# Score operands of a hybrid decoder step: which head's tiles the engines write and which the DMA moves fill, and when the cache copies are issued

## The chip, the cores and the metric

The kernel runs on one core of one Trainium2 chip. The metric is the device time of one execution in microseconds (us). The profile shows one further execution, engine by engine. The engines are TensorE (PE), VectorE (DVE), ScalarE (ACT), GpSimd (POOL) and SyncE (SP); here SP's queue issues all DMA transfers, in program order, and a transfer that has to wait holds up all that are behind it.

## The reference

One step of a one-layer decoder: 1024 prompt positions and 8 decode sequences, width 1024. One projection gives q, k and v of three dilated attention groups (8 heads of 64 each, dilations 1, 4 and 16), of one sliding-window group with a sink, and four gate paths. The caches, one position moved on, are outputs too.

```python
def layer_prompt(x, norm_gain, w_in, ...):
    a_qkv, (bq, bk, bv), gates = project_inputs(x, norm_gain, w_in, qk_norm_a, qk_norm_b)
    for g in range(A_GROUPS):                       # windows 128, 512, 2048; dilations 1, 4, 16
        q, k, v = a_qkv[g]
        o, lse = dilated_prompt(q, k, v, A_WINDOWS[g], A_DILATIONS[g])
        ...
    o_b, _ = banded_attention(bq, bk, bv, alibi_slopes(B_HEADS, 1), b_sinks, B_WINDOW, 1)
    y = merge_branches(x, jnp.stack(o_list), jnp.stack(lse_list), o_b, gates, w_branch_a, w_branch_b, w_out)

def decode_attention(q, cache_kv, k_new, v_new, n_keys, dil, slopes, sinks, window):
    kk = jnp.concatenate([cache_kv[:, :, 0], k_new], axis=1)
    ...
    new_kv = jnp.stack([kk[:, -keep:], vv[:, -keep:]], axis=2)      # the cache, moved on by one row

def merge_branches(x, o_a_groups, lse_a, o_b, gates, ...):
    wts = jax.nn.softmax(lse_a, axis=0)             # the three groups, by their softmax denominators
    o_a = jnp.einsum("gnth,gnthd->nthd", wts, o_a_groups)
    a = o_a.reshape(n, t, A_WIDTH) * jax.nn.silu(z_a)
    b = o_b.reshape(n, t, B_WIDTH) * jax.nn.silu(z_b)
    mixed = sigmoid(g_a) * (a @ w_branch_a) + sigmoid(g_b) * (b @ w_branch_b)
    return x + mixed @ w_out
```

## The kernel before

The work is a list of 82 weight tiles of 128 output columns (ORDER): gate tiles, then q, k and v tiles of the groups with gates between them, then the z tiles (58 to 65), the branch tiles (66 to 73) and the output tiles (74 to 81). Each tile is computed for 1032 columns (1024 prompt positions and 8 decode sequences) in three column blocks of 344. A column block is a slot of 24 matmuls, issued in three parts of 8 (line 248). Every operand is split into a high and a low part, and a product is high by high, high by low and low by high. The weights of tile n+2 are loaded by SP (line 118) while ACT and POOL split those of n+1 (lines 126 and 127).

Between the parts the program puts attention work: part_end runs what was put off by `after(parts, f)`, which means f runs that many parts later. A part is 8 projection matmuls plus the attention pieces put beside it, some 1.3 to 2 us. So the order of all queues is written out by these numbers, and nothing reorders it.

A q or k tile holds two heads, one in partitions 0 to 63 (lo_rows), the other in 64 to 127 (hi_rows). The score matmul of a head contracts over 128 partitions: a head's q tile holds its high part in one half and its low part in the other, and the k tiles are laid against it. So each part must be had by both heads' tiles, one in the place where it is written, the other by a DMA `move` of 64 partitions (256 KB, line 311; 128 KB in the dilation-16 group, line 348). prep_q fills q0 and q1 (both named q_st) for the two heads. prep_k fills, for head 0, a0 and b0, and for head 1, a1 and b1 (a named k_a and b k_b). It is used by the sliding-window group, once for all heads, and by the groups of dilation 1 and 4, once for each of their four tiles, nine times in all; prep_k2 does the same for dilation 16 with tiles k_st.

The score matmuls of a head against a and b are lines 448 and 449 (line 434 for dilation 16). One unit of score work is issued in every third part, all units of head 0 ahead of those of head 1: four units a head, two in the dilation-16 group. In stage_s line 457 (DVE) and line 467 (ACT) make the softmax numerators of a unit.

merge weighs the three groups of a head pair in four column quarters: DVE multiplies one group (line 726), POOL the other two and adds them (line 729), DVE adds the sum (line 731), and SP stores it (line 735). The z tiles read it back, and DVE multiplies it in (lines 1122, 1123). `yield n` lets n parts pass.

cache_copies moves the caches on by one row, from DRAM to DRAM, in 89 pieces: 64 of 1020 KB or a little more for the largest cache, 16 of that size for the next, 8 of 508 KB, and one of 1016 KB (line 145). slot issues one at the end of every second slot until they are used up, and a loop behind the last slot issues what is left. In the output tiles, ev_out loads the residual (xres, line 1172), DVE adds it (line 1174), and SP stores (line 1175).

Of the kernel before, what the change touches and what calls it, by code (L numbers as in the profile page):

```python
# [10 lines left out]
F32 = mybir.dt.float32  # L11
# [3 lines left out]
ALU = mybir.AluOpType  # L15
# [52 lines left out]
def hybrid_step(ctx: ExitStack, tc: tile.TileContext, a):  # L68
# [244 lines left out]
    def prep_q(j):  # L313

        j.sq = [rt("q_st") for _ in range(2)]
        t = rt("q_lo")
        q0, q1 = j.sq

        def piece(half):
            c = part_of(j, half)  # L320
            v = j.view(j.q[:, :T])[:, c]
            h = j.view_o(q0[:, :T])[:, c]
            nc.scalar.activation(h, v, AF.Copy)
            nc.gpsimd.tensor_tensor(j.view_o(t[:, :T])[:, c], v, h.bitcast(F32), op=ALU.subtract)  # L324
            if half:
                after(1, lambda: move(q1, lo_rows, q0, hi_rows))
                after(3, lambda: move(q1, hi_rows, t, hi_rows))
                after(3, lambda: move(q0, hi_rows, t, lo_rows))

        return [lambda: piece(0), lambda: piece(1)]  # L330

# [4 lines left out]
    def prep_k2(j):  # L336

        j.sk = [[rt("k_st") for _ in range(2)] for _ in range(2)]

        def piece(y):  # L340
            v = j.k[:, :T].rearrange("p (s r) -> p r s", r=16)[:, 8 * y:8 * y + 8].rearrange("p (b w) s -> p b w s", w=2)
            t0, t1 = [side(j.sk[h][y]) for h in range(2)]
            t4 = t0.rearrange("p b l (w s) -> p b l w s", s=64)
            nc.scalar.activation(t4[:, :, 0], v, AF.Copy)
            nc.vector.tensor_tensor(t4[:, :, 1], v, t4[:, :, 0].bitcast(F32), op=ALU.subtract)

            def mv(dst, d, l, src, s, m):
                nc.sync.dma_start(dst[d, :, l].bitcast(F32), src[s, :, m].bitcast(F32))

            after(1, lambda: mv(t1, lo_rows, 0, t0, hi_rows, 0))  # L350
            after(1, lambda: mv(t1, hi_rows, 1, t0, hi_rows, 0))
            after(2, lambda: mv(t1, lo_rows, 1, t0, hi_rows, 1))
            after(2, lambda: mv(t1, hi_rows, 0, t0, hi_rows, 1))
            after(5, lambda: mv(t0, hi_rows, 1, t0, lo_rows, 0))
            after(5, lambda: mv(t0, hi_rows, 0, t0, lo_rows, 1))

        return [lambda: piece(0), lambda: None, lambda: piece(1)]

    def prep_k(j):

        j.ka = [rt("k_a0"), rt("k_a1")]
        j.sk = [rt("k_b0"), rt("k_b1")]
        (a0, a1), (b0, b1) = j.ka, j.sk

        def piece(half):
            c = part_of(j, half)
            v = j.view(j.k[:, :T])[:, c]
            h = j.view_o(a0[:, :T])[:, c]
            nc.scalar.activation(h, v, AF.Copy)
            nc.vector.tensor_tensor(j.view_o(b0[:, :T])[:, c], v, h.bitcast(F32), op=ALU.subtract)  # L370
            if half:
                after(1, lambda: move(a1, lo_rows, a0, hi_rows))
                after(1, lambda: move(b1, hi_rows, a0, hi_rows))
                after(2, lambda: move(a1, hi_rows, b0, hi_rows))
                after(2, lambda: move(b1, lo_rows, b0, hi_rows))
                after(5, lambda: move(b0, hi_rows, a0, lo_rows))
                after(5, lambda: move(a0, hi_rows, b0, lo_rows))

        return [lambda: piece(0), lambda: None, lambda: piece(1)]

# [272 lines left out]
    def merge(c, js):  # L653
# [58 lines left out]
        for quarter in range(4):  # L712
            sc = scs[quarter]
            c0 = 256 * quarter
            for x, j in enumerate(js):
                if j.g == 1:
                    nv = j.n[:, :T].rearrange("p (r i) -> p i r", r=4)[:, 64 * quarter:64 * quarter + 64]
                    sv = sc[:, x].rearrange("p (i r) -> p i r", r=4)
                elif j.g == 2:
                    nv = j.n[:, :T].rearrange("p (r s) -> p s r", r=16)[:, 16 * quarter:16 * quarter + 16]  # L720
                    sv = sc[:, x].rearrange("p (s r) -> p s r", r=16)
                else:
                    nv = j.n[:, c0:c0 + 256]
                    sv = sc[:, x]
                eng = nc.vector if x == 0 else nc.gpsimd
                eng.tensor_tensor(nv if x == 0 else sv, nv, sv, op=ALU.mult)  # L726
            nv = js[0].n[:, c0:c0 + 256]
            if G == 3:
                nc.gpsimd.tensor_tensor(sc[:, 1], sc[:, 1], sc[:, 2], op=ALU.add)
                yield 2  # L730
                nc.vector.tensor_tensor(nv, nv, sc[:, 1], op=ALU.add)
            yield
            if quarter < 2:
                load(quarter + 2)
            nc.sync.dma_start(o_dr[oc, :, c0:c0 + 256], nv)
            yield 1
# [458 lines left out]
    def slot(n, ch):  # L1195
# [21 lines left out]
        else:  # L1217
            evac(n, ch, pt)
        part_end(in_att)
        if now[0] % 6 == 0 and now[0] > 18:  # L1220
            next(copies, None)

    n_tail = ORDER.index(("br", 0, 0))
# [254 lines left out]
```

## Time and profile before

| | |
|---|---|
| median of 3 runs | 1248.19 us (1246.03 to 1253.07) |
| profiled execution | 1248.59 us, its span 1246.0 us |
| busy: PE, ACT, DVE, POOL | 1181.5, 730.4, 707.0, 606.3 us |
| mean granted clock of PE | 0.977 of full speed |
| moved by DMA | 238.83 MB, 192 GB/s over the span |

Busy times are of the span of 1246.0 us. The span goes from the first to the last instruction; the profiled execution's own time has 2.6 us more around it. The granted clock is the share of full speed (2.4 GHz) that PE was given; its other level is half of it. The engine named behind an arrow in the profile is what ended a wait; "issue" stands where the profile shows nothing that did.

### The profile page before, as it was taken

Reading aid. Unit: us, or ns where it says so; the run is one execution under the profiler, and the core shown is the slowest. Engines: PE = TensorE matmul, PEld = TensorE weight load, DVE = VectorE, ACT = ScalarE, POOL = GpSimd, SP = SyncE. Lnnn points to the kernel's source line nnn. Section 1 sums busy time; section 2 is a strip of 40 time slices with the busy share of each in tenths; the row PEclk is TensorE's granted clock in tenths of the full one; section 3 lists DMA queues with packets and bytes.
Section 4 is the critical chain, followed back from the end, with each engine's and each line's share of the span. In section 5 each row is a group of like instructions: output and inputs, shape, how many; then the busy total and the mean of one; then the engine's idle time right before and its main releaser. Section 6 shows DMA issues by size and latency. Waiting matters only on the chain.

```text
span 1246.0 us, 21929 instructions
## 1 busy us (share of the span) xinstructions
PE 1181.5 (95%) x7625; PEld 1154.4 (93%) x7625; DVE 707.0 (57%) x1714; ACT 730.4 (59%) x1830; POOL 606.3 (49%) x681
## 2 busy tenths in 40 slices
PE   7899999999999998989998989989899999999998
PEld 6799999999899988979987989989899989999998
DVE  5852454676667475766755865757855564333111
ACT  5644675776758584758755677847686522443110
POOL 3554243443535455746363853638554685444220
PEclk9999999999999998989998989989999998999999
DMA  7047557675684849667775859486688754543343
GB/s 224 35 145 224 175 195 223 195 228 149 221 266 166 254 145 279 194 168 220 213 227 177 241 191 264 143 262 195 182 258 228 238 178 161 187 145 110 111 147 100
DMA packets 127278, 238.83 MB, mean 192 GB/s; under 512 B 28648, under 2 KB 102208, under 8 KB 125760
## 3 DMA queue, kind: packets, MB, share of 16 engines
q1 hardware_dynamic: 127168, 237.43, 62.3%
q8 instruction: 60, 0.98, 0.3%
q14 instruction: 50, 0.41, 0.1%
HBM read 180.14 MB, written 113.25 MB: 235 GB/s over the span
## 4 chain that ended last, share of the span: by engine, by line
PE 73%; DMA 7%; DVE 6%; POOL 5%; ACT 4%; issue 4%; SPq 1%; POOLq 0%; DVEq 0%; ACTq 0%
PE ps_d L248 55%; PE ps_w L248 4%; DMA k_a<-k_b 3%; PE ps_w L501 3%; PE ps_o L574 2%; PE ps_w L448 2%; PE ps_w L449 2%; DMA k_b<-k_b 2%; DMA w_st<-in_w 1%; ACT P L467 1%; PE ps_o L248 1%; DVE n_t L726 1%; POOL q_lo L324 1%; POOL n_t L591 1%; PE ps_w L950 1%
## 5 line engine op out<-in xcount | busy, mean ns | idle before, releaser
L248 PE MATMUL ps_d<-h_hi,w 128*128 128x344 f32 x3456 | 867.7, 327 | 12.2 <-DVE sq L1122 5.7
L248 PEld LDWEIGHTS ps_d<-h_hi,w 128*128 128x128 f32 x3456 | 611.7, 193 | 17.1 <-ACT h_hi L191 6.7
L248 PE MATMUL ps_d<-h_lo,w 128*128 128x344 f32 x1728 | 573.2, 332 | 5.9 <-POOL h_lo L221 3.3
L248 PEld LDWEIGHTS ps_d<-h_lo,w 128*128 128x128 f32 x1728 | 332.2, 192 | 10.6 <-POOL h_lo L221 5.8
L127 POOL TENSOR_TENSOR w<-w_st,w 128x512 fp32r<-128x512 f32 (+1 forms) x159 | 211.1, 1330 | 208.3 <-ACT w L126 193.4
L126 ACT ACTIVATE w<-w_st 128x512 fp32r<-128x512 f32 (+1 forms) x160 | 100.3, 631 | 113.3 <-DMA w_st<-in_w 112.5
L467 ACT ACTIVATE P<-P,st 128x256 f32<-128x256 f32 (+1 forms) x256 | 115.6, 453 | 65.6 <-DVE st L457 59.4
L956 POOL TENSOR_TENSOR qn<-qn,rn 128x344 f32<-128x344 f32 x48 | 45.6, 949 | 151.6 <-ACT rn L226 139.7
L528 DVE TENSOR_TENSOR pt<-ps_w,pt 128x384 fp32r<-128x384 f32 (+1 forms) x112 | 49.4, 441 | 57.7 <-ACT pt L527 57.3
L448 PE MATMUL ps_w<-k_a,q_st 128*128 128x128 f32 (+1 forms) x192 | 51.8, 293 | 29.0 <-DMA k_a<-k_b 14.6
L527 ACT ACTIVATE pt<-ps_w 128x384 fp32r<-128x384 f32 (+1 forms) x112 | 44.1, 394 | 42.8 <-DVE pt L528 36.0
L448 PEld LDWEIGHTS ps_w<-k_a,q_st 128*128 128x128 f32 x192 | 37.6, 196 | 31.0 <-issue 31.0
L501 PE MATMUL ps_w<-ident,P 128*128 128x128 f32 x400 | 62.3, 273 | 3.9 <-DVE pt L528 2.1
L956 POOL TENSOR_TENSOR kn<-kn,rn 128x344 f32<-128x344 f32 x39 | 37.0, 949 | 57.0 <-ACT rn L226 51.8
L941 ACT ACTIVATE sq<-ps_d 128x344 f32<-128x344 f32 x87 | 39.3, 452 | 39.8 <-PE ps_d L248 36.2
L946 DVE TENSOR_TENSOR sql<-sq,sqh 128x344 fp32r<-128x344 f32 x87 | 59.5, 684 | 0.8
L457 DVE CUSTOM_DVE_ANT_0 P<-ps_w,tab 128x256 f32<-128x256 f32 (+1 forms) x128 | 43.4, 375 | 27.4 <-PE ps_w L449 27.2
L501 PEld LDWEIGHTS ps_w<-ident,P 128*128 128x128 f32 x400 | 50.2, 140 | 7.1 <-issue 2.3
L792 POOL TENSOR_TENSOR dkv<-dkv,qb 128x512 f32<-128x512 f32 x32 | 42.4, 1331 | 28.0 <-DMA dkv<-in_ca 9.5
L1174 DVE TENSOR_TENSOR xres<-ps_d,xres 128x344 f32<-128x344 f32 x24 | 12.4, 517 | 76.1 <-PE ps_d L248 44.9
L230 DVE SCALAR_TENSOR_TENSOR ps_w<-ps_w,rt 128x344 f32<-128x344 f32 x87 | 45.2, 520 | 18.0 <-ACT rt L227 17.7
L449 PE MATMUL ps_w<-k_b,q_st 128*128 128x128 f32 (+1 forms) x192 | 53.1, 287 | 0.0
(226 smaller groups left out, 2064.7 us busy)
## 6 DMA issues: line engine op xcount, KB each, us to landing
w_st<-in_w SPq DMA_DIRECT2D x81, 512.0 KB
out_sa<-in_ca SPq DMA_DIRECT2D x16, 1020.0 KB
dkv<-in_ca SPq DMA_DIRECT2D x24, 512.0 KB
q_st<-q_lo SPq DMA_DIRECT2D x32, 256.0 KB
k_st<-k_st SPq DMA_DIRECT2D x48, 128.0 KB
sc<-sc_dr SPq DMA_DIRECT2D x32, 192.0 KB
k_b<-k_a SPq DMA_DIRECT2D x18, 256.0 KB
k_a<-k_b SPq DMA_DIRECT2D x18, 256.0 KB
```

The lines of the kernel that those rows point to most:

```text
L126: nc.scalar.activation(wh, s, AF.Copy)
L127: eng.tensor_tensor(wl, s, wh.bitcast(F32), op=ALU.subtract)
L230: nc.vector.scalar_tensor_tensor(ssq, ssq, n * EPS, t, op0=ALU.add, op1=ALU.mult)
L248: nc.tensor.matmul(pt[:, :CH], ops[i][0], ops[i][1], start=(i == 0), stop=(i == N - 1))
L448: nc.tensor.matmul(pt[:, o:o + 128 * nk], j.sq[h][:, q], j.ka[h][:, k], start=True, stop=False)
L449: nc.tensor.matmul(pt[:, o:o + 128 * nk], j.sq[h][:, q], j.sk[h][:, k], start=False, stop=True)
L467: nc.scalar.activation(u.p[:, c], u.p[:, c], AF.Exp, scale=-1.0, bias=st[:, qb, h:h + 1], accum_out=st[:, qb, 2 + h:3 + h])
L501: nc.tensor.transpose(pt[:, o:o + 128], u.p[:, o:o + 128], ident)
L527: nc.scalar.activation(t[:, p0:p0 + m], pt[:, o:o + m], AF.Copy)
L528: nc.vector.tensor_tensor(t[:, 512 + p0:512 + p0 + m], pt[:, o:o + m], t[:, p0:p0 + m].bitcast(F32), op=ALU.subtract)
L946: after(0, lambda: nc.vector.tensor_tensor(sl, s, sh.bitcast(F32), op=ALU.subtract))
L956: nc.gpsimd.tensor_tensor(dst[:, col], dst[:, col], r, op=ALU.mult)
```

## The change

In prep_q, prep_k and prep_k2 the tiles change roles: ACT's high part and the subtraction's low part are written to tiles of the second head (in prep_q the high part to a tile of its own, now q_hi), and the moves are turned about, so that the first four (in prep_q the first two) fill the first head's tiles and the last two (the last one) complete the second's. These last moves are issued 7 parts on instead of 5 (3 in prep_q). In merge the last add comes 3 parts behind POOL's instead of 2. The cache copies are issued every 9 parts up to tile 58 and every 6 parts from there on.

```diff
@@ def prep_q(j):
-        t = rt("q_lo")
+        t = rt("q_hi")
         q0, q1 = j.sq
...
-            h = j.view_o(q0[:, :T])[:, c]
+            h = j.view_o(t[:, :T])[:, c]
             nc.scalar.activation(h, v, AF.Copy)
-            nc.gpsimd.tensor_tensor(j.view_o(t[:, :T])[:, c], v, h.bitcast(F32), op=ALU.subtract)
+            nc.gpsimd.tensor_tensor(j.view_o(q1[:, :T])[:, c], v, h.bitcast(F32), op=ALU.subtract)
             if half:
-                after(1, lambda: move(q1, lo_rows, q0, hi_rows))
-                after(3, lambda: move(q1, hi_rows, t, hi_rows))
-                after(3, lambda: move(q0, hi_rows, t, lo_rows))
+                after(1, lambda: move(q0, lo_rows, t, lo_rows))
+                after(3, lambda: move(q0, hi_rows, q1, lo_rows))
+                after(7, lambda: move(q1, lo_rows, t, hi_rows))
@@ def prep_k(j):   (prep_k2 in the same way, with 7 for 5)
-            h = j.view_o(a0[:, :T])[:, c]
+            h = j.view_o(b1[:, :T])[:, c]
             nc.scalar.activation(h, v, AF.Copy)
-            nc.vector.tensor_tensor(j.view_o(b0[:, :T])[:, c], v, h.bitcast(F32), op=ALU.subtract)
+            nc.vector.tensor_tensor(j.view_o(a1[:, :T])[:, c], v, h.bitcast(F32), op=ALU.subtract)
             if half:
-                after(1, lambda: move(a1, lo_rows, a0, hi_rows))
-                after(1, lambda: move(b1, hi_rows, a0, hi_rows))
-                after(2, lambda: move(a1, hi_rows, b0, hi_rows))
-                after(2, lambda: move(b1, lo_rows, b0, hi_rows))
-                after(5, lambda: move(b0, hi_rows, a0, lo_rows))
-                after(5, lambda: move(a0, hi_rows, b0, lo_rows))
+                after(1, lambda: move(a0, lo_rows, b1, lo_rows))
+                after(1, lambda: move(b0, hi_rows, b1, lo_rows))
+                after(2, lambda: move(a0, hi_rows, a1, lo_rows))
+                after(2, lambda: move(b0, lo_rows, a1, lo_rows))
+                after(7, lambda: move(a1, lo_rows, b1, hi_rows))
+                after(7, lambda: move(b1, lo_rows, a1, hi_rows))
@@ merge, the last add of a quarter
-                yield 2
+                yield 3
                 nc.vector.tensor_tensor(nv, nv, sc[:, 1], op=ALU.add)
@@ def slot(n, ch):
-        if now[0] % 6 == 0 and now[0] > 18:
+        if now[0] % (9 if n < n_tail - 8 else 6) == 0 and now[0] > 18:
             next(copies, None)
```

SP's queue before, at the second k tile of the dilation-4 group (the numbers at k_a and k_b tell the tiles apart: 6313 and 6314 are a0 and a1, 6315 and 6316 are b0 and b1):

```order
L311 DMA k_a_6314<-k_a_6313 64x1024
L311 DMA k_b_6316<-k_a_6313 64x1024
L311 DMA k_a_6314<-k_b_6315 64x1024
L311 DMA k_b_6316<-k_b_6315 64x1024
L970 DMA out_pa<-v_t 128x512
L735 DMA o_dr<-n_t 128x256
L141 DMA out_sa<-in_ca 16x16384
L311 DMA k_b_6315<-k_a_6313 64x1024
L311 DMA k_a_6313<-k_b_6315 64x1024
L118 DMA w_st<-in_w 128x1024
```

The same place in the changed kernel (6296 and 6297 are a0 and a1, 6298 and 6299 are b0 and b1):

```order
L311 DMA k_a_6296<-k_b_6299 64x1024
L311 DMA k_b_6298<-k_b_6299 64x1024
L141 DMA out_sa<-in_ca 16x16384
L311 DMA k_a_6296<-k_a_6297 64x1024
L311 DMA k_b_6298<-k_a_6297 64x1024
L970 DMA out_pa<-v_t 128x512
L706 DMA sc<-sc_dr 64x3x256 x2
L735 DMA o_dr<-n_t 128x256
L311 DMA k_a_6297<-k_b_6299 64x1024
L311 DMA k_b_6299<-k_a_6297 64x1024
L118 DMA w_st<-in_w 128x1024
```

The first head's tiles are now filled by the first four moves instead of by the last two, a cache copy stands ahead of the third, and the one that stood ahead of the last two is gone.

The end of SP's queue before, the last two output tiles:

```order
L1172 DMA xres<-in_xT 128x1032
L1175 DMA out_yT<-xres 128x344 x3
L1172 DMA xres<-in_xT 128x1032
L1175 DMA out_yT<-xres 128x344 x3
L1474 UNCONDITIONAL_BRANCH
```

And in the changed kernel:

```order
L141 DMA out_sa<-in_ca 16x8128
L1172 DMA xres<-in_xT 128x1032
L1175 DMA out_yT<-xres 128x344 x2
L141 DMA out_sa<-in_ca 16x8128
L1175 DMA out_yT<-xres 128x344
L1172 DMA xres<-in_xT 128x1032
L1175 DMA out_yT<-xres 128x344
L141 DMA out_sa<-in_ca 16x8128
L1175 DMA out_yT<-xres 128x344 x2
L141 DMA out_sa<-in_ca 16x8128
L145 DMA out_sb<-in_cb 16x8x2032
L1474 UNCONDITIONAL_BRANCH
```

Copies of 508 KB now stand among the residual loads and stores, and the last two copies behind the last store.

## Rows read from the trace of the kernel before

**Rows 1.** The page: busy us and share by engine; DMA's busy tenths in 40 slices.
```profile
PE 1181.5 (95%) x7625; PEld 1154.4 (93%) x7625; DVE 707.0 (57%) x1714; ACT 730.4 (59%) x1830; POOL 606.3 (49%) x681
...
DMA  7047557675684849667775859486688754543343
```

**Rows 2.** PE's waits: line, releaser, us in total, times, longest.
```profile
PE ps_w L448 <- DMA k_a<-k_b: 14.6, 4, 6.0
PE ps_w L448 <- issue: 14.3, 4, 5.3
PE ps_d L248 <- DVE sq L1122: 5.7, 2, 3.0
```

**Rows 3.** PE's timeline at three of these waits: start, us, instruction, [idle before].
```profile
316.16 0.44 PE L448 MATMUL ps_w<-k_a,q_st 128*128 128x128 f32 x1 [2.99 <-DMA k_a<-k_b]
...
549.42 0.44 PE L448 MATMUL ps_w<-k_a,q_st 128*128 128x128 f32 x1 [6.00 <-DMA k_a<-k_b]
...
664.99 0.45 PE L448 MATMUL ps_w<-k_a,q_st 128*128 128x128 f32 x1 [5.31 <-issue]
```

**Rows 4.** SP's queue, timeline of 523 to 552 us.
```profile
533.72 0.60 SPq L311 DMA_DIRECT2D k_b<-k_b  x1
...
538.80 0.47 SPq L311 DMA_DIRECT2D k_b<-k_a  x1
539.36 1.53 SPq L311 DMA_DIRECT2D k_a<-k_b  x1
```

**Rows 5.** SP's queue, timelines of 300 to 312 and 648 to 668 us.
```profile
309.81 0.46 SPq L311 DMA_DIRECT2D k_b<-k_a  x1
...
652.86 0.60 SPq L311 DMA_DIRECT2D k_b<-k_b  x1
...
660.66 0.46 SPq L311 DMA_DIRECT2D k_b<-k_a  x1
```

**Rows 6.** SP's own waits, whole span: us in total, times, longest.
```profile
SPq L311 <- DMA k_b<-k_b: 24.2, 9, 6.3
```

**Rows 7.** Windows behind two waits; columns: us, PE, PEld, DVE, ACT, POOL, PEclk, DMA, GB/s.
```profile
491.75:498.75 7.00, 7.00 (x30) 6.61 (x31) 2.28 (x8) 2.65 (x8) 1.28 (x1) 0.63 0.87 329
834.73:839.73 5.00, 5.00 (x23) 5.00 (x24) 1.71 (x7) 1.69 (x6) 1.29 (x1) 0.66 1.10 447
```

**Rows 8.** The window of the wait that ends at 664.99.
```profile
660.00:665.00 5.00, 0.01 (x1) 0.04 (x1) 0.00 (x0) 0.49 (x1) 0.91 (x1) 0.92 0.64 154
```

**Rows 9.** SP's queue, timeline of 1040 to 1060 us: the last two copies.
```profile
1046.79 0.52 SPq L141 DMA_DIRECT2D out_sa<-in_ca  x1
1047.36 0.61 SPq L145 DMA_DIRECT2D out_sb<-in_cb  x1
```

**Rows 10.** Windows behind these copies.
```profile
1048.00:1050.00 2.00, 2.00 (x15) 2.00 (x14) 0.00 (x0) 0.39 (x1) 0.95 (x1) 1.00 1.16 451
1054.00:1056.00 2.00, 2.00 (x14) 2.00 (x14) 1.03 (x2) 0.82 (x3) 0.45 (x1) 1.00 0.00 0
```

**Rows 11.** SP's queue, timeline of 1243 to 1246 us.
```profile
1243.07 0.33 SPq L1175 DMA_DIRECT2D out_yT<-xres  x1
```

**Rows 12.** DVE's timeline of 1230 to 1246 us, the last output tile.
```profile
1236.18 0.52 DVE L1174 TENSOR_TENSOR xres<-ps_d,xres 128x344 f32<-128x344 f32 x1 [4.47 <-DMA xres<-in_xT]
1238.74 0.52 DVE L1174 TENSOR_TENSOR xres<-ps_d,xres 128x344 f32<-128x344 f32 x1 [2.04 <-PE ps_d L248]
```

**Rows 13.** SP's and ACT's timelines, 1090 to 1110 us: a gate's load and use.
```profile
1094.71 0.32 SPq L1149 DMA_DIRECT2D sg<-ga_dr  x1
...
1104.91 2.01 ACT L1155 ACTIVATE sg<-sg 128x1032 f32<-128x1032 f32 x2
```

**Rows 14.** DVE's timeline of 1005 to 1042 us, a multiply of the last merge.
```profile
1011.64 6.40 DVE L726 TENSOR_TENSOR n_t<-n_t,sc 128x256 f32<-128x256 f32 x1
```

**Rows 15.** PE's timeline of 1013 to 1020 us.
```profile
1018.51 0.43 PE L248 MATMUL ps_d<-h_hi,w 128*128 128x344 f32 x1 [2.97 <-DVE sq L1122]
```

**Rows 16.** The merge's last add, line 731: ns min/median/max; what its engine waited for.
```profile
L731 DVE TENSOR_TENSOR n_t<-n_t,sc x16: 404/792/3405, 514.8 to 1035.2; 128x256 f32<-128x256 f32 x16
...
  POOL sc L729: 2.9, 2
```

More of the change, by code (lines that the diff above doesn't have):

```diff
@@ L342, in piece @@
             t0, t1 = [side(j.sk[h][y]) for h in range(2)]
-            t4 = t0.rearrange("p b l (w s) -> p b l w s", s=64)
-            nc.scalar.activation(t4[:, :, 0], v, AF.Copy)
-            nc.vector.tensor_tensor(t4[:, :, 1], v, t4[:, :, 0].bitcast(F32), op=ALU.subtract)
+            t4 = t1.rearrange("p b l (w s) -> p b l w s", s=64)
+            nc.scalar.activation(t4[:, :, 1], v, AF.Copy)
+            nc.vector.tensor_tensor(t4[:, :, 0], v, t4[:, :, 1].bitcast(F32), op=ALU.subtract)
             def mv(dst, d, l, src, s, m):
                 nc.sync.dma_start(dst[d, :, l].bitcast(F32), src[s, :, m].bitcast(F32))
[L350 to L355, printed above, removed]
+            after(1, lambda: mv(t0, lo_rows, 0, t1, lo_rows, 1))
+            after(1, lambda: mv(t0, hi_rows, 1, t1, lo_rows, 1))
+            after(2, lambda: mv(t0, hi_rows, 0, t1, lo_rows, 0))
+            after(2, lambda: mv(t0, lo_rows, 1, t1, lo_rows, 0))
+            after(7, lambda: mv(t1, lo_rows, 0, t1, hi_rows, 1))
+            after(7, lambda: mv(t1, lo_rows, 1, t1, hi_rows, 0))
         return [lambda: piece(0), lambda: None, lambda: piece(1)]
```

## The prediction, made before the changed kernel was run

> **What bounds the kernel now.** I read the page first. TensorE (PE) is busy in 1181.5 of 1246.0 us and no other engine in more than 59% [rows 1], so the time falls only if PE's idle time falls or its clock rises. The profiled execution took 1248.59 us for its span of 1246.0 us, so 2.6 us lie around the span; the median of the runs is 1248.19 us, the same within 0.4 us, and the sum below is made from 1248.6.
>
> Next the waits of PE, longest first. The largest are two rows of one line, L448, the first score matmul of a head: 14.6 us in four waits put down to the move k_a<-k_b, and 14.3 us in four for which the view names no releaser [rows 2]. Together 28.9 us in eight waits, nearly half of PE's 64.5 us of idle time. To see what a wait "issue" is, I set PE's timeline against SP's queue, which issues the transfers. At 543.4 PE stops and goes on at 549.42, after 6.00 us [rows 3]. SP issued k_b<-k_b at 533.72, and the move that overwrites its source, k_b<-k_a, only at 538.80, when the former had landed; k_a<-k_b followed at 539.36 [rows 4] and landed as PE resumed, 10.1 us after its issue. That move fills the lower half of the *first* head's tile and is the sixth of six, the second link of a chain. At 664.99 ("issue", 5.31 us) it reads the same: k_b<-k_b issued at 652.86, its successor at 660.66, PE's restart 4 us after that [rows 3, 5]. The total of SP's waits for such a landing is 24.2 us in nine, one for each of the nine key tiles prepared this way [rows 6]. So I take all eight waits as the end of one chain: first move, wait, sixth move, landing.
>
> Last the clock. After such a stop PE runs at the lower of its two levels (1.2 instead of 2.4 GHz) for some us: the granted clock is 0.63 in the 7 us from 491.75 and 0.66 in the 5 us from 834.73, the restarts of two such waits [rows 7]. A stretch of length d at mean clock c loses d(1-c). Six of the eight restarts show it; stretches of 3 to 7 us, of which these are second and last, lose 13.4 us together.
>
> **What the change removes.** The ACT and DVE now write the second head's tiles directly, and the first head's tiles are filled by moves that read them and wait for no other move's landing. The moves on which the first score matmul waits are then the third and fourth, not the sixth. The number and size of moves is as before (3 for q, 6 for k).
> - *Idle, -29.0.* Where does PE stand instead? The fourth move (k_b<-k_b now) is issued at the same part of the program, so I take its landing from before: 538.80, 660.66 and 309.81 at the three sites shown [rows 4, 5]. PE arrives there at 543.4 (549.42-6.00), 659.7 (664.99-5.31) and 313.2 (316.16-2.99) [rows 3]. In the dilation-4 group the order of SP now has a cache copy of 1020 KB ahead of the third move: 1.04 MB at 451 GB/s [rows 10] is 2.3 us, plus 0.7 us of issue, so 541.8 and 312.8. Both are in time, the latter by 0.4 us; the site at 659.7 is late by 1.0 us. At the first use (129.7) and others I grant another 2. Residual +3, bounds 0 and 9.8 (a landing of 9.9 us for every fourth move).
> - *Clock, -13.4*, of which a residual wait may keep 1; bounds 0 and 13.4.
> - *Give-back, +4.* Work that used PE's stops must now fit beside it. In 660 to 665 DVE was busy 0.00 of 5 us and POOL 0.91 [rows 8]: they had nothing left to do, so a removed stop does not leave a backlog there. Bounds 0 and half of the 38 gained.
> - *Moves at +7 parts* fill the second head's tiles about two parts (some 3 us) later. That head starts 12 parts after the first (6 in the dilation-16 group), some 20 and 10 us, against landings of 5 to 10 us: nothing. Were that cover gone, they would bring back waits of 3 to 6 us.
>
> **Cache copies.** All 89 copies are issued as before, but 26 fewer ahead of tile 58. No PE wait is put down to a copy, so thinner traffic in the attention gains nothing by itself. The copies left over go behind: 12 beside the z tiles (as many as before), 12 beside the branch tiles, 12 beside the output tiles, and the last two (508 and 1016 KB) behind the last output store.
> - *After the last store, +5.* The store was issued at 1243.07 and ended the span [rows 11]. The 1016 KB copy was issued at 1047.36, behind a copy of 508 KB, and no byte moved from 1054.0 on: 6.6 us [rows 9, 10]. Issued at about 1244.1 it ends near 1250.7, 4.7 us beyond the old end, with the same closing steps behind. Bounds 3.5 (1.56 MB at 451 GB/s, [rows 10]) and 6. The Trainium skill, page DMA: Bandwidth & Descriptors, section Where 436 GB/s comes from, gives some 358 GB/s of HBM traffic per core; reading and writing 1.56 MB would by that estimate take 8.7 us, and the sum would be 4 us higher. The row of 451 GB/s, in which copied bytes count once, does not agree, so I leave that figure out.
> - *Beside the output tiles, +1.* Each output tile loads its residual, and DVE's first add waits for it; the next add still waits 2.04 us for PE [rows 12]. The copy directly ahead of three of these loads costs 2.3 us (1020 KB) or 1.2 us (508 KB): at most 0.3 us past that slack. Bounds 0 and 7 (three full copies).
> - *Beside the branch tiles, 0.* A gate's load issued at 1094.71 is used by ACT at 1104.91 [rows 13]; a copy of 2.3 us ahead leaves it in time. Without that cover each 1020 KB copy would cost 2.3 us.
>
> **The merge** waits one part longer ahead of DVE's last add. In the dilated merges DVE stood 2.9 us in all at that add for POOL [rows 16], with no PE wait put down to it; each merge ends four parts later. 0; bounds are a rival below.
>
> **Sum.** 1248.6 - 29.0 + 3 - 13.4 + 1 + 4 + 5 + 1 = 1220.2. I forecast 1220 us, 2.2% faster, likeliest range 1211 to 1231.
>
> **Rivals.**
> 1. *The single moves land late too.* In the dilation-4 group the copy stands ahead of them now, and k_a<-k_b took 10.1 us though little else moved. For: the landing of 7.8 us at 652.86 behind a copy [rows 5]. Against: PE arrives 3 to 10 us later than those landings at most sites. With 9.9 us everywhere 9.8 us of waits stay instead of 3, and half the clock loss: 1220 + 7 + 6 = 1233.
> 2. *Give-back.* The other engines become the bound where DVE and POOL are crowded. For: PE also waits for DVE today, 5.7 us at L1122 alone [rows 2]. Against: rows 8. With half of 38 us given back: 1220 - 4 + 19 = 1235.
> 3. *The merge collides with POOL.* One DVE multiply of the last merge took 6.40 us where POOL worked without a gap, and behind it PE stood 2.97 us [rows 14, 15]; with its twin at 1032 and the low clock after both that is 10.7 us. The moved add itself took 404 to 3405 ns [rows 16]. A shift by a part could remove this (1209) or double it (1231). The Trainium skill, page SBUF — State Buffer, section Who interferes with whom, has DVE instructions with two SBUF inputs shut out while GpSimd reads SBUF, as long as its instruction lasts; by that rule the later add stays exposed, and these rows agree that DVE is held.
> 4. *Half of it is something else.* The four waits without a named releaser hang on another thing, and stay: 14.3 us less residual, and their dips of 7.3 us: 1220 + 22 = 1242.
> 5. *Slower: the tail cannot hold the copies.* 24 copies now go beside the branch and output tiles, 16 of 2.3 us and 8 of 1.2 us, 46 us in all. If PE waits for each in full it is 1220 + 45 = 1265; the sign turns when more than six tenths of their time holds PE up. Against: rows 12 and 13, slack of 2 us and more in both places, in a stage where the engines of the transfers are busy for 3 to 5 tenths [rows 1].
>
> **How the numbers follow.** The forecast has 0.57, rival 1 0.13, rival 2 0.08, rival 3 0.10 (half to each side), rival 4 0.05, rival 5 0.07. 0.5%, some 6 us, is about what a measurement can tell from no change: faster is below 1242, slower above 1254. Faster gathers the forecast and rivals 1 to 3, less a little for their upper ends, 0.86; same is rival 4 and those ends, 0.07; slower 0.07. The range takes in the forecast with its lower bounds and rivals 1 to 3: 1206 to 1241, leaving out rivals 4 and 5 and the lowest few.
>
> **What would show it.** Right: L448 all but gone from PE's waits (under 6 us); SP's waits for k_b<-k_b shorter; PE's clock above 0.985; the last store some 25 to 30 us earlier, and behind it 5 us of copies alone. Wrong: L448 still waiting 10 us or more for a move (rival 1 or 4), new PE waits for DVE or POOL of that size (2, 3), or PE waiting for residual or weight loads behind tile 66 (5).

## The result: 0.6% slower, and the profile after

The changed kernel took 1257.41 us (median of 20 runs, 1253.54 to 1259.91) against 1249.84 us for the kernel before in the same session: a ratio of 1.0059, 95% interval 1.0045 to 1.0074. The forecast was 1220 us. The profiled execution has a span of 1254.3 us in place of 1246.0.

First the page: the busy line, and of the 40 slices the rows of PE and of the DMA engines (answers to [rows 1]).

```profile
PE 1182.8 (94%) x7625; PEld 1147.7 (91%) x7625; DVE 700.5 (56%) x1714; ACT 727.2 (58%) x1830; POOL 604.2 (48%) x681
...
PE   7899999999999999979999999999899989999997
...
DMA  6146446563673739666666657576587776785765
```

PE is as busy as before, and not idle less: 1254.3 - 1182.8 = 71.5 us against 64.5. The last slice of PE is thinner, and the DMA engines now work to the end. So the stops that the change took away came back elsewhere. Where, PE's waits say (line, releaser: us in total, times, longest):

```profile
PE ps_w L951 <- DVE sql L946: 12.6, 11, 4.6
...
PE ps_w L950 <- ACT sqh L945: 3.8, 3, 1.3
...
PE ps_w L448 <- DMA q_st<-q_st: 2.3, 1, 2.3
...
PE ps_w L448 <- DVE mrow L695: 0.5, 1, 0.5
...
PE ps_w L449 <- DMA k_b<-k_a: 0.3, 1, 0.3
```

The 28.9 us at L448 of [rows 2] are 2.8 us now, 3.1 with its partner L449, as forecast. In their place PE stands at L950 and L951, the two matmuls that sum the squares for the norm of q and k, and waits for ACT and DVE, 16.4 us; before the change that was 0.6 us. To see what makes those two engines late I set ACT's timeline beside PE's at one of three places that look alike (543, 717 and 883 us; start, length, engine and line, operation and tiles, and in brackets the idle time before it with its releaser):

```profile
543.59 0.60 ACT L392 ACTIVATE v<-ps_w 128x512 fp32r<-128x512 f32 x1 [3.07 <-PE ps_o L574]
544.08 0.45 ACT L941 ACTIVATE sq<-ps_d 128x344 f32<-128x344 f32 x1
544.57 0.49 ACT L945 ACTIVATE sqh<-sq 128x344 fp32r<-128x344 f32 x1
```

```profile
545.11 0.42 PE L950 MATMUL ps_w<-sqh,blk 128*128 128x344 f32 x1 [1.26 <-ACT sqh L945]
545.87 0.43 PE L951 MATMUL ps_w<-sql,blk 128*128 128x344 f32 x1 [0.34 <-DVE sql L946]
...
553.05 0.43 PE L951 MATMUL ps_w<-sql,blk 128*128 128x344 f32 x1 [1.40 <-DVE sql L946]
...
562.84 0.66 PE L951 MATMUL ps_w<-sql,blk 128*128 128x344 f32 x1 [4.62 <-DVE sql L946]
```

```profile
558.99 3.79 DVE L946 TENSOR_TENSOR sql<-sq,sqh 128x344 fp32r<-128x344 f32 x1
```

ACT stands 3.07 us ahead of L392, the copy of the second half of v, until PE's L574, a matmul of the job before that multiplies softmax numerators with v (a PV matmul), is done. The diff does not touch v. Behind L392 on ACT stand the square and its rounding, so PE, which had no reason to wait, waits for them (1.26 and 0.34 us, within 0.01 the same at all three places). The longest stop, 4.62 us at 562.84, is at the first place alone, and there DVE's subtraction took 3.79 us, where it mostly takes 0.51. What ties v to the old PV matmul is its slot. All big tiles share 18 slots, and a tile that is given back later changes which slot the tiles behind it get. The addresses in the built programs show that the change dealt them anew:

```
second half of v in the three later dilation-4 jobs: the tile that held its slot last
kernel before    n_t           n_t           n_t          (a merged tile, long read)
changed kernel   v (1st half)  v (1st half)  v (1st half) (of the job before: L574 still reads it)
```

On SP's queue the waits for landings have grown, not shrunk (28.9 us for q_st and, in [rows 6], 24.2 for the key tiles before), and those for a residual's load too (27.1 us before):

```profile
SPq L311 <- DMA q_st<-q_st: 59.9, 15, 6.0
SPq L1175 <- DMA xres<-in_xT: 36.2, 8, 6.4
SPq L311 <- DMA k_b<-k_a: 29.5, 8, 5.9
```

Last the tail, SP's queue near two of the output tiles and at the end, and DVE's first add of the former:

```profile
1175.11 0.52 SPq L141 DMA_DIRECT2D out_sa<-in_ca  x1
1175.67 0.58 SPq L1172 DMA_DIRECT2D xres<-in_xT  x1
...
1242.08 4.12 SPq L1175 DMA_DIRECT2D out_yT<-xres  x2
1246.24 0.52 SPq L141 DMA_DIRECT2D out_sa<-in_ca  x1
1246.80 0.61 SPq L145 DMA_DIRECT2D out_sb<-in_cb  x1
```

```profile
1182.75 0.94 DVE L1174 TENSOR_TENSOR xres<-ps_d,xres 128x344 f32<-128x344 f32 x2 [8.05 <-DMA xres<-in_xT]
```

A cache copy stands right ahead of a residual's load, which lands 7 us after its issue, and DVE waits 8.05 us. Two copies stand behind the last store: PE's last matmul ends at 1245.28, 9.0 us ahead of the span's end, where it was 1242.49 and 3.5.

### The profile page after: what moved, and what is told of

Its sections match the earlier page's. It is cut to its first block, busy times and chain, and to the rows that moved or that the text cites. A ratio compares the mean times of both kernels' runs of the same rounds, so it can differ in the third digit from the quotient of the medians.

```text
span 1254.3 us, 21916 instructions
## 1 busy us (share of the span) xinstructions
PE 1182.8 (94%) x7625; PEld 1147.7 (91%) x7625; DVE 700.5 (56%) x1714; ACT 727.2 (58%) x1830; POOL 604.2 (48%) x681
## 4 chain that ended last, share of the span: by engine, by line
PE 62%; DMA 12%; ACT 8%; DVE 8%; POOL 4%; issue 3%; SPq 2%; DVEq 0%; POOLq 0%; ACTq 0%
PE ps_d L248 47%; PE ps_w L248 3%; PE ps_w L501 3%; DMA w_st<-in_w 3%; DMA k_b<-k_a 2%; PE ps_o L574 2%; ACT P L467 1%; PE ps_w L448 1%; PE ps_w L449 1%; DMA q_st<-q_st 1%; DVE dpr L911 1%; DMA xres<-in_xT 1%; DMA sc<-sc_dr 1%; PE ps_o L248 1%; PE ps_w L951 1%
## 5 line engine op out<-in xcount | busy, mean ns | idle before, releaser
L467 ACT ACTIVATE P<-P,st 128x256 f32<-128x256 f32 (+1 forms) x256 | 115.5, 452 | 69.9 <-DVE st L457 64.5
L946 DVE TENSOR_TENSOR sql<-sq,sqh 128x344 fp32r<-128x344 f32 x87 | 59.8, 687 | 0.7
L448 PE MATMUL ps_w<-k_a,q_st 128*128 128x128 f32 (+1 forms) x192 | 50.7, 286 | 2.8 <-DMA q_st<-q_st 2.3
L449 PE MATMUL ps_w<-k_b,q_st 128*128 128x128 f32 (+1 forms) x192 | 52.5, 285 | 0.4 <-DMA k_b<-k_a 0.3
L324 POOL TENSOR_TENSOR q_st<-qn,q_hi 128x512 fp32r<-128x512 f32 x32 | 45.3, 1428 | 11.7 <-ACT q_hi L323 10.3
L225 ACT ACTIVATE rn<-ps_w,eps 128x344 f32<-128x344 f32 x89 | 47.8, 537 | 4.4 <-PE ps_w L205 4.0
```

The costliest lines, as they stand in the source:

```text
L225: nc.scalar.activation(r, ssq, AF.Ln, scale=1.0 / n, bias=eps)
L324: nc.gpsimd.tensor_tensor(j.view_o(q1[:, :T])[:, c], v, h.bitcast(F32), op=ALU.subtract)
L448: nc.tensor.matmul(pt[:, o:o + 128 * nk], j.sq[h][:, q], j.ka[h][:, k], start=True, stop=False)
L449: nc.tensor.matmul(pt[:, o:o + 128 * nk], j.sq[h][:, q], j.sk[h][:, k], start=False, stop=True)
L467: nc.scalar.activation(u.p[:, c], u.p[:, c], AF.Exp, scale=-1.0, bias=st[:, qb, h:h + 1], accum_out=st[:, qb, 2 + h:3 + h])
L946: after(0, lambda: nc.vector.tensor_tensor(sl, s, sh.bitcast(F32), op=ALU.subtract))
```

## The experiments

Four theories went into them. **A, slots**: the merge ends later, gives n_t back later, and v takes a slot that PE still reads. **B, port**: DVE's work only fell anew against POOL's. **C, copies**: the loss is the copies'. **D**: the exchange of roles moves the wait to what is queued behind the moves. Each run was timed beside the kernel before (1249 to 1250 us in every session); ratios are to it, with 95% intervals.

### Slot or place of the add: three runs

**e1** is the changed kernel with the merge back at two parts:

```
-                yield 3
+                yield 2
```

> The changed kernel with the merge's wait put back from three parts to two. Theory A (slots): the longer merge gives back the tile n_t four parts later, so the second half of v in the three later dilation-4 jobs takes the slot that the last PV matmuls of the job before still read; ACT stands 3.1 to 3.7 us there for L574, and PE loses 3 us of idle time (1.27, 0.34 and 1.41 us) at each of three sites, with the low clock behind it some 12 us in all. With two parts v takes a merged n_t tile again: the wait of L392 for L574 (9.8 us in 3) is gone, and the time is 12 us below the changed kernel's 1257, near 1245. Theory B (port): the later add only shifted DVE's collisions with POOL, so about the same 12 us but with the L392 wait still there. Theory C (copies and tail hold the loss): no change, 1257.

**e2** keeps the three parts, but drops the pause of one part at the end of each quarter of a dilated merge, so that the merge ends when it used to:

```
             nc.sync.dma_start(o_dr[oc, :, c0:c0 + 256], nv)
-            yield 1
+            if G < 3:
+                yield 1
```

> The changed kernel, where each quarter of a dilated merge drops its last pause of one part, so that DVE's last add stays at three parts but the merge ends as early as before the change. Theory A (slots): v takes the merged tile again, L392 does not wait for L574, near 1245. Theory B (the place of the add against POOL): the add is where it was in the changed kernel, so near 1257. Theory C (copies and tail): 1257.

**e3** is e1 with the dilated merge started four parts later, so that it ends when the changed kernel's does:

```
-        yield 5
+        yield 5 if isb else 9
```

> The changed kernel with the add back at two parts, but the dilated merge started four parts later (nine parts after its loads in place of five), so that n_t is given back as late as in the changed kernel and v takes the slot of the v before it. Theory A (slots): L392 waits for L574 again, some 3 us in each of three jobs, near 1257. Theory B (place of the add): as with the add at two parts, near 1245. Theory C: 1257.

Measured: e1 1248.78 us (1.0021, 1.0000 to 1.0043), e2 1246.36 (0.9982, 0.9955 to 1.0009), e3 1259.49 (1.0099, 1.0067 to 1.0131). In the built programs v has n_t's slot in e1 and e2 and the old v's in e3. ACT's waits in e3 have the row again, which neither e1 nor e2 has:

```profile
ACT v L392 <- PE ps_o L574: 10.5, 3, 3.8
```

So it is the late return of the slot, as A has it: with the changed kernel's 1.0059 the late returns stand 0.78% above the early ones at either place of the add, some 10 us. Matched matmul by matmul, the changed kernel loses 4, 5 and 6 us to e1 at the three places where ACT stands for L574, and 6 us more at the stop before 562.84, where the subtraction ran beside POOL's work; it makes up a part of that elsewhere. The add's place by itself goes the other way: three parts are 0.4% below two at either return, each time just clear of the noise. So B falls as a theory of the add's place, but a late return also costs by where DVE's work then falls against POOL's.

### The parts alone: six runs

**e4** leaves only the exchange of roles (the merge at two parts as in e1, the copies every six parts):

```
-        if now[0] % (9 if n < n_tail - 8 else 6) == 0 and now[0] > 18:
+        if now[0] % 6 == 0 and now[0] > 18:
```

> Only the exchange of roles in the three preparations; merge wait two parts and copies every six parts as in the kernel before. Theory A: the first-head waits (29 us) and their low clock are gone, v takes merged tiles, no copy is left for the end: near 1238, 10 to 13 us below the kernel before. Theory C (copies held the loss): 1225 or less. Theory D (the exchange itself only moves the wait: SP stands 95 us for landing moves in place of 53, and what is queued behind them comes late): no better than the kernel before, 1245 to 1250.

The next four are the kernel before with one part of the change's diff each. **e5** has only the copies' spacing:

> The kernel before with only the copies' wider spacing. From the roles alone (1236) to roles with copies (1249) the time rose 13 us: 5.5 us behind the last store and some 6 us in the output tiles 75 to 78, where a copy of 1020 KB stands on SP's queue ahead of a residual's load. Theory A (the tail alone): the same 12 us here, near 1260, and nothing gained in the attention. Rival (thinner traffic lets the preparation's moves land earlier, and pays back a part where PE waits for them): the waits at L448 shrink, 1250 or less.

**e7** has only `yield 3`:

> The kernel before with only the merge's wait of three parts. Here the later return of n_t gives v's second half in the dilation-4 jobs the slot of a v_t, last read by transposes long before. Theory A (slots): no wait of L392 for L574, and so no loss: 1247 to 1251. Rival (a later add and a merge that ends four parts later cost by themselves): near 1258, as the changed kernel against the same with two parts.

**e11** has only the exchange in `prep_k` and `prep_k2`, **e12** only that in `prep_q`:

> Only the exchange in the two preparations of k; q as before, copies and merge as before. The eight waits of 29 us at L448 were put down to the sixth move of k. Theory K (all the gain comes from k): 1236, as with all roles exchanged, or a few us less if the q exchange holds SP up (q_st landing waits). Rival (q's exchange is needed too, its chain of three moves is next in line): L448 waits for q_st by several us, 1241 to 1247.

> Only the exchange in the preparation of q. Theory K: the waits at L448 for k_a stay as they were (29 us), 1248 or a few us more. Rival (a part of those waits was q's): they fall by 5 us or more, 1238 to 1244.

**e6** is e1 with the copies every three parts behind tile 50, so that none is left for the output tiles:

```
-        if now[0] % (9 if n < n_tail - 8 else 6) == 0 and now[0] > 18:
+        if now[0] % (9 if n < n_tail - 8 else 3) == 0 and now[0] > 18:
```

> Roles and wide copies with the merge at two parts (1249), where the copies come every three parts in place of six behind tile 50, so that the last of them goes beside the fifth branch tile and none beside the output tiles or behind the last store. Theory A (the copies cost only where they stand ahead of a residual load or behind the last store): back to the time of the roles alone, 1236 to 1238. Rival (wide spacing in the attention has a cost of its own, or 38 copies in the z and branch tiles hold up gate loads and stores): 1242 to 1250.

| run | what is in it | us | ratio | interval |
|---|---|---|---|---|
| e11 | k's exchange | 1230.63 | 0.9853 | 0.9819 to 0.9888 |
| e12 | q's exchange | 1255.70 | 1.0055 | 1.0033 to 1.0078 |
| e5 | copies | 1263.28 | 1.0100 | 1.0066 to 1.0134 |
| e7 | merge at three parts | 1254.07 | 1.0041 | 1.0019 to 1.0064 |
| e4 | k's and q's exchange | 1235.67 | 0.9911 | 0.9876 to 0.9946 |
| e6 | e4 and copies, ending early | 1250.65 | 1.0016 | 0.9997 to 1.0035 |

The parts add up: -1.47 + 0.55 + 1.00 + 0.41 = +0.49%, and the whole change has +0.59%. Only k's exchange gains. Each part deals the slots anew as well: of the pool's 232 tiles 141 lie elsewhere in e11 than in the kernel before, 134 in e5 and 105 in e7. So a price in this table includes what the new slots cost or save.

*Copies.* From e4 to e1 they cost 1.1%. Matched matmul by matmul the two are within 4 us of each other, and level at the start of tile 75; in tiles 75 and 76 e1 loses 6.6 us, nearly all of it at one residual's load, and its span ends 5.5 us later behind the last matmul than e4's. So C holds for some 12 us, and thinner traffic in the attention gains nothing. In e6 the copies stand ahead of a gate's load instead, which waits as the residuals do (ACT's first use of the gate, and PE behind it); some 10 us are lost there and 6 in the z tiles:

```profile
1066.67 1.06 ACT L1155 ACTIVATE sg<-sg 128x1032 f32<-128x1032 f32 x1 [10.79 <-DMA sg<-ga_dr]
```

```profile
1068.34 0.66 PE L248 MATMUL ps_d<-ab_hi,w 128*128 128x344 f32 x1 [7.01 <-DVE mx L1161]
```

*q.* In e12 SP stands 6.8 us on the second move of k near 345 until the second head's L449 of an earlier job is done (the slot of k_b again came from a tile that is still read), and PE stops where the kernel before does not:

```profile
SPq L311 <- PE ps_w L449: 6.8, 1, 6.8
```

```profile
367.28 0.44 PE L448 MATMUL ps_w<-k_a,q_st 128*128 128x128 f32 x1 [4.66 <-DMA k_a<-k_b]
```

*Merge alone.* e7 lost 5 us where A said none: v has the slot of a v_t there and does not wait for L574. But it waits at two of the three places for the store that still reads v_t:

```profile
ACT v L392 <- DMA out_pa<-v_t: 5.8, 2, 3.1
```

So a late return cost ACT time here too, by another reader of the slot. PE's rows show 3.7 us more at L543 for DVE and 3 us more at L448; whether ACT's wait moved them was not tried.

### Where half of k's gain stays: nine runs

Aligned matmul by matmul and counted from the stop to 5 us behind the restart, e11 gains 37 us at six of the eight sites of [rows 2], where the forecast took 42 of waits and clock for all, and yet ends only 15 us ahead. What gives the rest back? In e4 and e11 the longest new stop is at L951 near 556 to 562. DVE, POOL and PE of e11 there:

```profile
555.21 6.45 DVE L946 TENSOR_TENSOR sql<-sq,sqh 128x344 fp32r<-128x344 f32 x1
```

```profile
554.67 1.28 POOL L127 TENSOR_TENSOR w<-w_st,w 128x512 fp32r<-128x512 f32 x1
555.92 1.05 POOL L903 TENSOR_TENSOR dkv<-dkv,sco 128x512 f32<-128x512 f32 x1
556.94 0.91 POOL L956 TENSOR_TENSOR kn<-kn,rn 128x344 f32<-128x344 f32 x1
557.81 0.18 POOL L1012 COPY dc<-qn 128x8 f32<-128x8 f32 x1
557.96 0.39 POOL L906 TENSOR_TENSOR rw<-rw,sls 8x128 f32<-8x128 f32 x1
558.31 2.97 POOL L324 TENSOR_TENSOR q_lo<-qn,q_st 128x512 fp32r<-128x512 f32 x2
```

```profile
561.72 0.66 PE L951 MATMUL ps_w<-sql,blk 128*128 128x344 f32 x1 [4.11 <-DVE sql L946]
```

The same subtraction mostly takes 0.51 us. Here it lasts 6.45 us, while one POOL operation follows another without a gap. Two runs on e4 move a split from one of the two engines to the other (e8: the low part of q, L324, to DVE; e9: the low part of k, L370, to POOL):

```
-            nc.gpsimd.tensor_tensor(j.view_o(q1[:, :T])[:, c], v, h.bitcast(F32), op=ALU.subtract)
+            nc.vector.tensor_tensor(j.view_o(q1[:, :T])[:, c], v, h.bitcast(F32), op=ALU.subtract)
```

> Only the exchange of roles (1236), with the low part of q taken by DVE in place of POOL (L324, 32 instructions of 1.43 us, 45 us of POOL's time, some 34 us more for DVE at the 1.07 us of L345). With the roles alone 29 us of PE's waits at L448 went and some 15 us came back behind DVE: one subtraction of L946 took 6.45 us and two of L370 4.4 and 4.7 us while POOL worked without a gap (L324 among it), and PE stood 4.1 us. Theory P (the give-back is DVE held by POOL): those long ones shrink, PE's waits for DVE sql and pt fall by 5 us or more, 1228 to 1233. Theory T (DVE and ACT are simply late, more work on DVE makes it worse): 1238 to 1245.

```
-            nc.vector.tensor_tensor(j.view_o(a1[:, :T])[:, c], v, h.bitcast(F32), op=ALU.subtract)
+            nc.gpsimd.tensor_tensor(j.view_o(a1[:, :T])[:, c], v, h.bitcast(F32), op=ALU.subtract)
```

> Only the exchange of roles (1236), with the low part of k (L370, 18 instructions of 1.14 us on DVE, stretched to 4.4 and 4.7 us in two) taken by POOL, at some 1.43 us each. The reverse move, q's low part from POOL to DVE, made it 11 us slower, so DVE's load is a suspect. Theory T (the give-back is DVE late for PE): 20 us less on DVE, PE's waits for DVE pt and sql fall, 1226 to 1233. Rival (the chain of the preparation is what counts, POOL's 1.43 us and its queue make the moves late again): L448 waits for a move, 1238 to 1245.

e8 took 1248.14 us (0.9986, 0.9963 to 1.0009), e9 1248.83 (0.9991, 0.9968 to 1.0014). Both lose what the roles had gained. With e8, whose tiles lie as in e4, the long L946 near there shrank to 3.0 us and PE's stop behind it from 4.1 to 0.7, and yet the time rose by other waits for DVE, so this collision is not the bulk. In e9 PE stood 21.3 us at L387 for DVE, but that was a slot again:

```profile
POOL k_a L370 <- PE ps_w L449: 25.5, 3, 9.4
```

In the built program the second head's first key tile (a1) of the three later dilation-4 jobs has the slot of the same tile of the job before, which L449 still reads. POOL stands there, and DVE's add of the merge behind it. So e9 does not say whether DVE's load is what gives the gain back; e8, where more of it made things worse, leaves that open.

**e10** is e4 with all last moves at ten parts (on q and k); **e13** the same on e11, k alone:

```
-                after(7, lambda: move(a1, lo_rows, b1, hi_rows))
-                after(7, lambda: move(b1, lo_rows, a1, hi_rows))
+                after(10, lambda: move(a1, lo_rows, b1, hi_rows))
+                after(10, lambda: move(b1, lo_rows, a1, hi_rows))
```

> Only the exchange of roles, with the moves that fill the second head's tiles at ten parts in place of seven. They still come some ten parts ahead of that head's first scores. With seven parts SP stands 49 us (26.5 for q_st, 22.8 for k_b) until the earlier move that reads what the next overwrites has landed, and all that is queued behind on SP (weight, scale and cache loads) stands with it. Theory S (that block of SP is part of the give-back): SP's waits fall below 15 us and the time to 1228 to 1232. Rival (SP's stands are covered): SP's waits fall, the time stays at 1234 to 1238.

> k's exchange alone (1231) with its last moves at ten parts in place of seven. Theory S (SP's stands of 22 us for k_b landings hold up what is queued behind): 1224 to 1228. Rival (those stands are covered by the time that the queue has anyway): 1229 to 1233, with SP's wait for k_b halved all the same.

e10: 1234.12 us (0.9890, 0.9862 to 0.9918), not to be told from e4. e13: **1214.39 us (0.9705, 0.9672 to 0.9738)**, 16 us below e11 and far past its expectation. In the built programs e13's tiles have the same addresses as e11's to the end of the attention, while 90 of 232 differ between e10 and e4 (q_hi is held longer): in e13 the moves' time is all that changed. e13's rows (PE, ACT, SP), and those of e11 beneath:

```profile
PE ps_w L951 <- DVE sql L946: 1.8, 4, 0.6
...
ACT w L126 <- DMA w_st<-in_w: 93.4, 26, 10.3
...
SPq L311 <- DMA k_b<-k_a: 7.9, 2, 5.4
```

```profile
PE ps_w L951 <- DVE sql L946: 9.0, 7, 4.1
...
ACT w L126 <- DMA w_st<-in_w: 117.9, 26, 10.6
...
SPq L311 <- DMA k_b<-k_a: 22.2, 7, 6.1
```

At seven parts the last two moves, which overwrite what earlier ones still read, stand 22.2 us on SP, and ACT waits 24.5 us longer for weights that are loaded behind them. SP's order near 530 shows it (e11, then e13, which is 11 us ahead by then):

```profile
536.69 0.47 SPq L311 DMA_DIRECT2D k_a<-k_b  x1
537.25 0.58 SPq L311 DMA_DIRECT2D k_b<-k_a  x1
537.88 1.43 SPq L118 DMA_DIRECT2D w_st<-in_w  x1
```

```profile
525.05 0.54 SPq L118 DMA_DIRECT2D w_st<-in_w  x1
...
530.10 0.54 SPq L311 DMA_DIRECT2D k_a<-k_b  x1
530.68 1.32 SPq L311 DMA_DIRECT2D k_b<-k_a  x1
```

**e17** asks whether the weight load is the cause: e11 with the load issued two parts earlier, moves still at seven.

```
-                after(5, lambda: w_load(n + 2))
+                after(3, lambda: w_load(n + 2))
```

> k's exchange alone, last moves at seven parts as in the change, but every weight load issued at three parts of a tile in place of five, so that it stands on SP ahead of those moves and not behind them. Theory W (the 18 us between seven and ten parts are the weight load that stands behind the moves: ACT waits for it at L126, 118 us in all against 93): ACT's wait at L126 falls to 100 us or less and the time to 1214 to 1222. Rival (something else that is queued behind the moves, or SP now standing for POOL at the earlier load): 1228 to 1236.

1229.45 us (0.9858, 0.9810 to 0.9907), no better than e11, though ACT's wait for weights fell further than in e13. SP now stands for POOL instead (177.1 us in e11), and PE at L951 as before:

```profile
ACT w L126 <- DMA w_st<-in_w: 39.9, 16, 8.2
...
SPq L118 <- POOL w L127: 263.5, 50, 14.6
...
PE ps_w L951 <- DVE sql L946: 9.2, 9, 4.1
```

So the weight load alone is not the explanation, or its gain was lost to the new stand.

**e14** and **e16** break POOL's run with a pause between the halves of q's preparation, on e11 and on e13:

```
-        return [lambda: piece(0), lambda: piece(1)]
+        return [lambda: piece(0), lambda: None, lambda: piece(1)]
```

> k's exchange alone (1231) with a pause of one part between the two halves of q's preparation, so that POOL's two L324 no longer follow each other without a gap. Theory P (DVE's subtraction L946 lasts as long as POOL works without a gap): the 6.45 us L946 near 555 shrinks to 5 or less, PE's stop of 4.1 us behind it to 2.5 or less, and the time by 2 to 6 us, 1225 to 1229. Rival (the length of that one has another cause, or the pause makes k's moves late by a part): no shorter, 1230 to 1236.

> k's exchange alone with both, last moves at ten parts and the pause in q's preparation. If both theories hold 1220 to 1226; if neither, 1229 to 1236.

e14: 1229.96 us (0.9840, 0.9808 to 0.9872), the long L946 at 4.99 us, PE's stop 2.7: the stop shrinks about as expected, the time by no more than can be told. e16: 1218.14 (0.9740, 0.9705 to 0.9775), nothing beyond e13.

**e15** is e12 (q alone) with its last move at three parts, where q_lo was given back before the change; **e18** is all three exchanges with q's last move at three and k's at ten:

```
-                after(7, lambda: move(q1, lo_rows, t, hi_rows))
+                after(3, lambda: move(q1, lo_rows, t, hi_rows))
```

> Only q's exchange (1256), with its last move issued at three parts, as before the change, in place of seven, so that q_hi is given back as early as q_lo was. Theory A (slots: the longer life of q_hi gives later key tiles other slots, and a move then stands on SP for 7 us near 345): that stand is gone and the time is that of the kernel before, 1247 to 1251. Rival (q's exchange costs by its own moves, of which the last now waits for a landing at once and blocks SP): 1255 or more.

> All three exchanges, k's last moves at ten parts, q's last move at three, merge and copies as before the change. If q's exchange adds nothing of its own: 1212 to 1217, as k's alone at ten parts. If its last move at three parts, which waits for a landing at once (71 us of SP's stands in the run with q alone), holds up the weight loads: 1219 to 1228.

e15: 1251.15 us (0.9998, 0.9970 to 1.0025), so q's 7 us are gone, and with them SP's stand near 345 and PE's stop at 367: the key tile that waited has q_hi's slot there in place of an older key tile's. e18: 1212.17 us (0.9719, 0.9674 to 0.9764), level with e13; q's exchange adds nothing. Its rows go against a simple form of D:

```profile
SPq L311 <- DMA q_st<-q_st: 70.7, 16, 7.6
```

SP stands 79 us for landings there (70.7 and 8.6), against 54 in e11 and 49 in e4, and it is one of the two fastest. Nor does less of them help each time: in e10 SP's stands fell to 8.4 us and ACT's wait for weights to 93.6, as in e13, and the time stayed. So stands on SP do not cost by their sum; that it matters which part of a tile they fall on is a guess. What exactly the last moves of k hold up at seven parts stays open: it is in their place on SP, since nothing else differs between e11 and e13, but neither the weight load nor POOL's run accounts for the 18 us alone. What they cost shows: of the 23 us between the two profiled spans 14 are idle time of PE (54.5 and 40.4 us), mostly in short waits for DVE and ACT, and the granted clock is 0.986 and 0.991.

## Why the prediction was wrong, step by step

The runs make a ladder from the best version to the changed kernel, and each rung is a step of the forecast:

| step | forecast, us | measured, us | from |
|---|---|---|---|
| waits and clock at L448 removed, with residual and give-back | -34.4 | -36.9 | e13 |
| moves at seven parts | 0 | +18.5 | e11 less e13 |
| q's exchange | 0 | +7.2 | e4 less e11 |
| copies | +6 | +13.7 | e1 less e4 |
| merge | 0 | +4.7 | changed less e1 |
| sum | -28.4 | +7.2 | |

(Measured: differences of the ratios times 1249 us, each uncertain by 3 to 6 us. Each is the price of its step on top of the steps above it, with the slots that go with it.)

- *What the change removes* was right in size, and in cause for seven of the eight waits. Counted as for e11 (37 us), the six sites gain 36 us in the changed kernel too, and 37 in e13; the forecast had 38 (29.0 - 3 + 13.4 - 1) for all eight. The wait at 129.73 was not the key moves': the last of them was issued at 98.73, the last q_st<-q_lo at 123.66. The wait stays in e13, where q's moves are as before, and is gone in e12, where they are turned about (the kernel before, then e13):

```profile
129.73 0.30 PE L448 MATMUL ps_w<-k_a,q_st 128*128 128x128 f32 x1 [2.62 <-issue]
```

```profile
129.19 0.30 PE L448 MATMUL ps_w<-k_a,q_st 128*128 128x128 f32 x1 [2.20 <-DMA q_st<-q_lo]
```

So rival 4 falls but for these 2.6 us. Residual: 3.1 us, against 3, of which 2.3 are q's. Rival 1 falls with it. The mean granted clock goes from 0.977 before to 0.984 in the changed kernel and 0.991 in e13, so its part of the gain was real, and partly spent on the new stops.
- **The step that failed first is "Moves at +7 parts ... nothing".** It asked only whether the second head's tiles are filled in time. They are (PE waits 0.3 us in all for a k_b<-k_a). But with k's exchange alone the same moves are 18 us faster at ten parts, at the same tile addresses. At seven parts they overwrite rows that earlier moves read, wait on SP for their landing (22.2 us), and have the weight load behind them. SP stood as long for this in the kernel before (24.2 us [rows 6]), so the stand by itself is no new cost, and how the place of these moves costs PE time stays open.
- *q's exchange* got no term of its own, and *the merge* was costed at nothing with the sentence "each merge ends four parts later" beside it. Both prices go with slots: a tile held longer changes which old tile every later one waits for. Late return of n_t costs 10 us (e1, e2, e3 and the changed kernel), of q_hi 7 us (e12, e15). Rival 3 looked at the merge for another reason, POOL's port; the later add itself came out 5 us faster with either return.
- *Copies.* "After the last store, +5" was right: 9.0 less 3.5 is 5.5 us. The output tiles cost some 6 us and not 1, near their upper bound of 7, and nearly all at one load and not at three: the slack of 2.04 us of [rows 12] was taken as that of every tile, and the load behind a copy came 7 us after its issue, not 2.3 us late.
- *Give-back, +4*, argued from [rows 8]: DVE idle in a stop was taken to mean nothing is left to do. In e13, with the stops gone, that holds. At seven parts it does not: e11 gains 37 us at the six sites and ends 15 ahead, so some 20 are given back, the size of rival 2 (19). Rival 2 has the picture of the changed kernel right too (PE waits for ACT and DVE, 16.4 us at L950 and L951). Its cause, too much work beside the stops, was not shown: late slots are a part, and in e13 the same work fits.
- Rival 5 had the sign, by the tail; its mechanism gave 12 us of the 46 that it could have had. None of the rivals was a slot.

## What to carry to other kernels

Where tiles share a pool, compare the waits of the rows that a diff does *not* touch: here v's copy lost its wait for POOL and kept one on PE alone, which stood in the program's order before any run and says that its slot has a new owner. When a move is shifted, ask of each queue that it stands in not only whether its own data come in time, but what is queued behind it while it waits to overwrite. And time the parts of a bundle apart: one of five here carried all the gain, and the four others, each held to be free or nearly so, cost 44 us.

## What the runs showed of the hardware

One DVE subtraction with both inputs in SBUF took 6.45 us in e11, where it mostly takes 0.51, and spanned the six POOL operations from 555.92 to 561.28, which followed each other without a gap; it ended during the next one, L916. In e13 POOL ran the same operations in the same order without a gap, and there the subtraction got in earlier, during the small copy L1012 (544.70 to 545.17):

```profile
542.49 2.63 DVE L946 TENSOR_TENSOR sql<-sq,sqh 128x344 fp32r<-128x344 f32 x1
```

The Trainium skill, page SBUF — State Buffer, section Who interferes with whom, says that such an instruction contends with a GpSimd instruction that reads SBUF, and, of DVE's 2-port modes, that whoever issues first gets the shared pair of ports for its whole instruction. The rows agree that DVE is held. In e11 it was held over several POOL operations in a row, in e13 over fewer, and no run here shows what decides how many.
